# Short convolutions in token form: tap rows on VectorE and adding DMAs for the neighbour tokens

## The chip, the core and the metric

The kernel runs on one core of a Trainium2 chip. The metric is the device time of one execution in microseconds. Engines are named as the profile names them: PE (TensorE) multiplies matrices, DVE (VectorE) and ACT (ScalarE) work elementwise, POOL (GpSimd) and SP (SyncE) issue DMAs here. Each engine works through its own instructions in order.

## The reference

One encoder block over 256 tokens with 2048 channels. Two branches, gated linear attention (GLA) and a second-order Hyena operator, are gated and summed, projected, normalised, and followed by a squared-ReLU MLP. What the change touches is the start of the Hyena branch: a convolution over three neighbouring tokens for each of 6144 channels, split into v, x1 and x2.

```python
proj = h @ w_in[l]
q, k, v, r, af, ab, hy_u, gate_logits = jnp.split(proj, split_idx, axis=-1)

def _short_conv(u, w, b):          # w: (3, 6144): previous, own, next token
    y = lax.conv_general_dilated(u, w[:, None, :], (1,), [(1, 1)], ...)
    return y + b

uc = _short_conv(hy_u, conv_w, conv_b)
v, x1, x2 = jnp.split(uc, 3, axis=-1)
z = v
for o, gate in enumerate((x1, x2)):
    zc = long_convolution(z, filt[:, o])      # by FFT over 2 * 256 points
    z = gate * (zc + skip[o] * z)

merged = g0 * (y_gla @ w_gla_o) + g1 * (z @ w_hy_o)
```

## The kernel before

Activations and weights are split into a high and a low part (fp32r), and each product is the sum of three: high by high, high by low, low by high. Weights come as 305 blocks of 1 MB; `fetch` loads a block on SP's queue and splits it in two halves, high on ACT (line 84), low on DVE (line 85). Three raw blocks and three halves of each part (`whi`, `wlo`) are kept.

There are two forms of a product of 256 tokens with a block of weights. In channel form (`channel_pair`, lines 145 and 149) the weights are stationary and the result has channels on the partitions: a block gives 128 channels with 16 products 512 wide (high and low part of the activations side by side) and 16 products 256 wide. `channel_sum` (lines 157, 158) then adds the two parts: ACT takes one out of PSUM, DVE adds the other. In token form (`token_group`, lines 204 to 206) the activations are stationary and the result has tokens on the partitions: four blocks give 512 channels, with 24 products 512 wide each, straight into two PSUM tiles, one for each half of the tokens. PSUM has four such tiles in turn, so the two of one group are written again two groups later.

`pump` counts the blocks, and `later(d, f)` puts a step of the Hyena branch into the program d counts on. A scheduler then orders each engine's instructions.

The convolution stage goes over eight chunks of 256 channels. For each it makes uv, ux and uz as channel pairs of xT (tags v, x1, x2), and `short_conv` (lines 704 to 706) convolves along the free dimension, where the neighbour token is one column away: ACT scales the own token and adds the bias, DVE adds the two neighbours. v and x1 are then turned into token form by four PE transpositions each (`to_tokens`, line 713); v is split in high and low, x1 is copied out of PSUM. `hy_fwd` transforms (Zp) and loads the filter (Tl, on POOL's queue), `hy_mul` multiplies by it on DVE (Z, pa, pb, lines 754 to 760), `hy_inv` transforms back (yp), and gates with x1 in token form (line 776). After the second order the result is copied out, transposed back to channels (yT, line 786), gated with x2 in channel form (line 788), and stored to DRAM (yd, on POOL's queue), from where `reload` fetches it later. After every second chunk there is one token group of the GLA output projection (`go`). Then come the second gate (g2) and the Hyena output projection (ho).

Of the kernel before, what the change touches and what calls it, by code (L numbers as in the profile page):

```python
# [42 lines left out]
def block_kernel(  # L43
# [5 lines left out]
    wa2: bass.AP,  # L49
    ba: bass.AP,  # L50
    norm_g: bass.AP,
    convp: bass.AP,
    mlp_w: bass.AP,
    mlp_c: bass.AP,
    emb: bass.AP,
# [24 lines left out]
    def psum_side(name):  # L80
        return sdp.tile([P, 512], F32, tag="sd", name=name)

    def split_hi_lo(hi, lo, src):
        return (nc.scalar.copy(hi, src),  # L84
                nc.vector.tensor_tensor(lo, src, hi.bitcast(F32), op=ALU.subtract))  # L85
# [151 lines left out]
    conv_sb = base.tile([P, 48, 4], F32, tag="convp", name="conv_sb")  # L237
# [97 lines left out]
    def mm3(ps, lh, ll, rh, rl, start, stop):  # L335
        MM(ps, lh, rl, start=start, stop=False)
        MM(ps, lh, rh, start=False, stop=False)
        MM(ps, ll, rh, start=False, stop=stop)
# [8 lines left out]
    def filt_consts():  # L347
        raw = fp.tile([P, 4, P], F32, tag="w4", name="dftraw")
        nc.gpsimd.dma_start(raw, dft_in)
        split_hi_lo(dfth, dftl, raw)  # L350
        mw = fp.tile([P, 3, P], F32, tag="mlpw", name="mlpw")
        nc.gpsimd.dma_start(mw, mlp_w)
        mc = fp.tile([P, 4], F32, tag="mlpc", name="mlpc")
        nc.gpsimd.dma_start(mc, mlp_c)
        et = fp.tile([P, L], F32, tag="emb", name="emb_sb")
        nc.gpsimd.dma_start(et, emb)
        nc.gpsimd.dma_start(ba_sb, ba)
        nc.gpsimd.dma_start(conv_sb, convp)
# [337 lines left out]
    cst = {}  # L696
    yh_dram = {}

    def short_conv(ps, base_ct, name, tag, bufs):
        y = hp.tile([P, 2, L], F32, tag=tag, bufs=bufs, name=name)  # L700
        for c in range(2):
            cp = conv_sb[:, base_ct + c, :]
            u = ps[:, c]
            nc.scalar.activation(y[:, c, :], u, AF.Identity, scale=cp[:, 1:2], bias=cp[:, 3:4])
            nc.vector.scalar_tensor_tensor(y[:, c, 1:L], u[:, 0:L - 1], cp[:, 0:1], y[:, c, 1:L], op0=ALU.mult, op1=ALU.add)
            nc.vector.scalar_tensor_tensor(y[:, c, 0:L - 1], u[:, 1:L], cp[:, 2:3], y[:, c, 0:L - 1], op0=ALU.mult, op1=ALU.add)
        return y

    def to_tokens(src, name):
        pt = psum_side(name)  # L710
        for c in range(2):
            for tb in range(NT):
                nc.tensor.transpose(pt[:, tb * CW + c * P:tb * CW + (c + 1) * P], src[:, c, tb * P:(tb + 1) * P], ident)
        return pt.rearrange("p (a b) -> p a b", a=2)

    def z_tiles(name):
        return (hp.tile([P, NT, CW], F32R, tag="zh", bufs=2, name=f"zh{name}"),
                hp.tile([P, NT, CW], F32R, tag="zl", bufs=2, name=f"zl{name}"))
# [8 lines left out]
    def hy_x1(c):  # L727
        def run():
            x1 = hp.tile([P, NT, CW], F32, tag="x1", name=f"x1_{c}")
            nc.scalar.copy(x1, to_tokens(cst.pop(("x1c", c)), f"x1t{c}"))  # L730
            cst[("x1", c)] = x1
        return run

    def hy_fwd(c, o):
        def run():
            t = hp.tile([P, 2, 3, CW], F32, tag="Tl", name=f"Tl{c}{o}")
            nc.gpsimd.dma_start(t, T_dram[(c, o)])
            zh, zl = cst.pop(("z", c, o))
            z = hp.tile([P, 3, 2, CW], F32, tag="Z", name=f"Z{c}{o}")
            for ri in range(2):  # L740
                pz = psum_side(f"Zp{c}{o}{ri}")
                mm3(pz, dfth[:, ri], dftl[:, ri], zh, zl, True, True)
                nc.scalar.copy(z[:, 2:0:-1, ri, :], pz.rearrange("p (a b) -> p a b", a=2))
            cst[("Z", c, o)] = (t, z)
        return run
# [21 lines left out]
    def hy_inv(c, o):  # L767
        def run():
            yh, yl = cst.pop(("Y", c, o))
            py = psum_side(f"yp{c}{o}")  # L770
            py3 = py.rearrange("p (a b) -> p a b", a=2)
            mm3(py3, dfth[:, 2], dftl[:, 2], yh[:, :, 0], yl[:, :, 0], True, False)
            mm3(py3, dfth[:, 3], dftl[:, 3], yh[:, :, 1], yl[:, :, 1], False, True)
            if o == 0:
                zf = hp.tile([P, NT, CW], F32, tag="zf", name=f"zf{c}")
                nc.vector.tensor_tensor(zf, py3, cst.pop(("x1", c)), op=ALU.mult)
                z = z_tiles(f"{c}1")
                split_hi_lo(z[0], z[1], zf)
                cst[("z", c, 1)] = z
            else:  # L780
                zf = hp.tile([P, NT, CW], F32, tag="zf", name=f"zg{c}")
                nc.scalar.copy(zf, py3)
                pt = psum_side(f"yT{c}")
                for cc in range(2):
                    for tb in range(NT):
                        nc.tensor.transpose(pt[:, cc * L + tb * P:cc * L + (tb + 1) * P], zf[:, tb, cc * P:(cc + 1) * P], ident)
                yo = hp.tile([P, 2, L], F32, tag="zf", name=f"yo{c}")
                nc.vector.tensor_tensor(yo, pt.rearrange("p (a b) -> p a b", a=2), cst.pop(("x2", c)), op=ALU.mult)
                if c == NCH - 1:
                    split_hi_lo(yhT[:, 2 * c:, 0], yhT[:, 2 * c:, 1], yo)  # L790
                    return
# [12 lines left out]
        for tb in range(NT):  # L804
            nc.vector.tensor_tensor(mg[:, tb], mg[:, tb], pss[tb], op=ALU.mult)

    go_after = [0, 1, 0, 1, 0, 1, 0, 1]
    for c in range(NCH):
        ps = channel_pair(xT, f"uv{c}")
        cst[("v", c)] = short_conv(ps, 2 * c, f"cv{c}", "cv", 2)  # L810
        later(2, hy_v(c))
        later(4, hy_fwd(c, 0))
        later(4, hy_mul(c, 0))
        ps = channel_pair(xT, f"ux{c}")
        cst[("x1c", c)] = short_conv(ps, 16 + 2 * c, f"cx{c}", "cx", 1)
        later(2, hy_x1(c))
        later(6, hy_inv(c, 0))
        later(7, hy_fwd(c, 1))
        later(7, hy_mul(c, 1))
        ps = channel_pair(xT, f"uz{c}")  # L820
        cst[("x2", c)] = short_conv(ps, 32 + 2 * c, f"cz{c}", "cz", 2)
        later(9, hy_inv(c, 1))
        for _ in range(go_after[c]):
            gla_o_group()


    yhT = act_tile(base, "yT", "yh")

    def reload(c):
        def run():  # L830
            yr = hp.tile([P, 2, L], F32, tag="cv", bufs=2, name=f"yr{c}")
# [4 lines left out]
    for c in range(NCH - 1):  # L836
        later(c, reload(c))
# [289 lines left out]
def _layout(a):  # L1127
# [18 lines left out]
        seg[n] = w_in[:, s:s + z]  # L1146
        s += z
    ga = np.concatenate([seg["af"], seg["ab"]] * 4, axis=1)
    u = chan(seg["u"]).reshape(3, NCH, 2, P, D)
    go = tok(a["w_gla_o"][0])  # L1150
    ubl, gi = [], 0
    for c, n in enumerate([0, 1, 0, 1, 0, 1, 0, 1]):
        for t in range(3):
            ubl.append(u[t, c])
        ubl.append(go[gi:gi + 4 * n])
        gi += 4 * n
    f1 = chan(a["w_ff1"][0])
    w2 = a["w_ff2"][0]
    f1q = [f1[16 * i:16 * (i + 1)] for i in range(QT)]
# [18 lines left out]
    cw = a["hy_conv_w"][0].reshape(3, 48, P).transpose(2, 1, 0)  # L1178
    convp = np.concatenate([cw, a["hy_conv_b"][0].reshape(48, P).T[:, :, None]], axis=2)
# [22 lines left out]
    for r0 in (0, 32):  # L1202
# [32 lines left out]
    sc[:, 0::64] = 0.0  # L1235
    return {
        "x": a["x"][0], "first": first, "wblk": wblk, "wa2": wa2, "ba": ba, "norm_g": a["gla_norm_g"],
        "convp": convp, "mlp_w": mlp_w, "mlp_c": mlp_c, "emb": emb, "w4s": w4s,
        "ln_rows": ln_rows, "ln_turn": ln_turn, "ident_in": np.eye(P, dtype=f), "dft_in": dft,
        "sgn_in": sgn, "l2c_in": l2c, "decay_in": decay, "mask_in": mask, "scan_in": sc,  # L1240
    }
# [17 lines left out]
```

## Time and profile before

| | |
|---|---|
| median of 3 runs | 1856.17 us (1856.01 to 1856.2) |
| the profiled execution's own time | 1856.49 us |
| its span | 1854.7 us |
| instructions | 23944 |
| start of the first uv product | 457.3 us |
| start of the first go product | 531.4 us |
| start of the last uz product | 836.5 us |
| start of the last ho product | 1043.3 us |

A row of a group gives the line, engine and operation, output and inputs by the program's names, their shapes and how often it ran; then the busy time of the group and the mean of one instruction in ns; then the engine's idle time just before them and what ended it. The mean of a product is longer than the distance to the next one, since products are pipelined; distances are read from the start times of the timeline. A row of time windows gives, for each engine, busy time and instructions, then the granted clock of PE, the busy share of the DMA engines and GB/s. A row of waits gives who waited for whom, the total, how often and the longest. A row of DMA issues gives the size of one and the median time from issue to landing; a row of queues gives packets, MB and the time of its packets as a share of 16 engines' span.

### The profile page before, as it was taken

To read this page: it belongs to the slowest core of one execution; us is meant where nothing else is said; L and a number is where in the kernel's file an instruction comes from. 1 tells how busy PE (TensorE), PEld (TensorE's weight loads), DVE (VectorE), ACT (ScalarE), POOL (GpSimd) and SP (SyncE) were. 2 spreads that over 40 slices of the span, in tenths; PEclk is the share of its full clock that TensorE was granted. 3 is DMA by queue.
4 is the path that set the end of the run, shared out by engine and by line. 5 is a ranking of instruction groups with operands and counts; after the bars stand their busy time and mean duration, and the time that the engine had idled before them with its cause. 6 is when DMAs were issued, how large, how long until landed. Compare 5 with 4: busy or idle time off the path is not lost.

```text
span 1854.7 us, 23944 instructions
## 1 busy us (share of the span) xinstructions
PE 1846.9 (100%) x9447; PEld 1570.9 (85%) x9447; DVE 1286.3 (69%) x1642; ACT 935.9 (50%) x1270; POOL 29.7 (2%) x59
## 2 busy tenths in 40 slices
PE   9999999999999999999999999999999999999999
PEld 7888888888888888888888889888888888888887
DVE  6888878765788988888645567666555655665567
ACT  6656558665555555555444445444434443444332
POOL 1000000000000000000000000000000000000000
PEclk9999999999999999999999999999999999999999
DMA  8577664435555555556555764455554555555553
GB/s 317 215 250 272 239 243 169 162 136 201 196 199 202 194 205 193 207 207 227 181 203 183 277 225 167 182 214 194 182 199 187 194 192 185 201 183 193 191 191 127
DMA packets 59377, 374.99 MB, mean 202 GB/s; under 512 B 6689, under 2 KB 9153, under 8 KB 20097
## 3 DMA queue, kind: packets, MB, share of 16 engines
q1 hardware_dynamic: 46080, 324.03, 47.6%
q0 software_dynamic: 6128, 29.64, 4.3%
q10 hardware_dynamic: 7056, 19.80, 3.0%
q8 instruction: 74, 1.21, 0.3%
q14 instruction: 39, 0.31, 0.0%
HBM read 356.92 MB, written 16.52 MB: 201 GB/s over the span
## 4 chain that ended last, share of the span: by engine, by line
PE 97%; DVE 1%; ACT 1%; DMA 0%; issue 0%; SPq 0%; DVEq 0%
PE f L145 12%; PE f L149 6%; PE w L206 6%; PE w L205 6%; PE w L204 6%; PE uz L145 3%; PE uv L145 3%; PE ux L145 3%; PE g L205 3%; PE g L206 3%; PE g L204 3%; PE uv L149 2%; PE ux L149 2%; PE uz L149 2%; PE k L145 2%; PE r L206 2%
## 5 line engine op out<-in xcount | busy, mean ns | idle before, releaser
L85 DVE TENSOR_TENSOR wlo<-raw,whi 128x1024 fp32r<-128x1024 f32 x584 | 712.3, 1222 | 358.8 <-ACT whi L84 356.4
L84 ACT CAST whi<-raw 128x1024 fp32r<-128x1024 f32 x584 | 613.4, 1051 | 484.4 <-PE w L206 188.0
L145 PE MATMUL f<-hT,whi 128*128 128x512 f32 x984 | 235.1, 391 | 0.0
L145 PEld LDWEIGHTS f<-hT,whi 128*128 128x128 f32 x984 | 180.8, 188 | 35.0
L205 PE MATMUL w<-wlo,f 128*128 128x512 f32 x480 | 186.7, 389 | 0.0
L206 PE MATMUL w<-whi,f 128*128 128x512 f32 x480 | 186.7, 389 | 0.0
L204 PE MATMUL w<-whi,f 128*128 128x512 f32 x480 | 167.4, 389 | 0.0
L149 PEld LDWEIGHTS f<-hT,wlo 128*128 128x128 f32 x984 | 126.2, 191 | 4.8
L149 PE MATMUL f<-hT,wlo 128*128 128x256 f32 x984 | 127.7, 283 | 0.0
L157 ACT ACTIVATE f_l<-f 128x256 f32<-128x256 f32 x64 | 24.5, 384 | 162.2 <-PE f L145 159.3
L205 PEld LDWEIGHTS w<-wlo,f 128*128 128x128 f32 x480 | 90.1, 188 | 18.7
L204 PEld LDWEIGHTS w<-whi,f 128*128 128x128 f32 x480 | 90.1, 188 | 18.7
L206 PEld LDWEIGHTS w<-whi,f 128*128 128x128 f32 x480 | 90.1, 188 | 18.7
L205 PE MATMUL g<-wlo,xT 128*128 128x512 f32 x256 | 100.0, 391 | 0.6 <-DVE wlo L85 0.6
L158 DVE SCALAR_TENSOR_TENSOR f_s<-f,f_l 128x256 f32<-128x256 f32 x64 | 27.2, 425 | 105.1 <-ACT f_l L157 105.1
L206 PE MATMUL g<-whi,xT 128*128 128x512 f32 x256 | 99.7, 389 | 0.0
L204 PE MATMUL g<-whi,xT 128*128 128x512 f32 x256 | 92.4, 390 | 0.0
L145 PE MATMUL uz<-xT,whi 128*128 128x512 f32 x256 | 63.7, 393 | 0.0
L145 PE MATMUL ux<-xT,whi 128*128 128x512 f32 x256 | 63.6, 391 | 0.0
L145 PE MATMUL uv<-xT,whi 128*128 128x512 f32 x256 | 63.1, 391 | 0.0
L205 PEld LDWEIGHTS g<-wlo,xT 128*128 128x128 f32 x256 | 48.1, 188 | 10.9 <-DVE wlo L85 1.1
L204 PEld LDWEIGHTS g<-whi,xT 128*128 128x128 f32 x256 | 48.1, 188 | 9.9
(438 smaller groups left out, 3223.2 us busy)
## 6 DMA issues: line engine op xcount, KB each, us to landing
raw<-wblk SPq DMA_DIRECT2D x300, 1024.0 KB, 4.8
Td<-T POOLq DMA_DIRECT2D x16, 768.0 KB, 4.2
Tl<-Td POOLq DMA_DIRECT2D x16, 768.0 KB, 4.6
w<-w4s ACTq DMA_DIRECT2D x16, 512.0 KB, 4.7
xw<-first SPq DMA_DIRECT2D x5, 896.0 KB, 12.9
zr<-ln_rows ACTq DMA_DIRECT2D x4, 1024.0 KB, 10.8
xw<-first SPq DMA_DIRECT2D x6, 448.0 KB, 7.2
dec<-decay_in ACTq DMA_DIRECT2D x8, 256.0 KB, 3.7
```

The costliest lines, as they stand in the source:

```text
L84: return (nc.scalar.copy(hi, src), nc.vector.tensor_tensor(lo, src, hi.bitcast(F32), op=ALU.subtract))
L85: nc.vector.tensor_tensor(lo, src, hi.bitcast(F32), op=ALU.subtract))
L145: MM(ps[:, :, ts], hi[:, js], act[:, kt, :, ts], start=(kt == 0 and opens), stop=(kt == KT - 1))
L149: MM(ps[:, 0, ts], lo[:, js], act[:, kt, 0, ts], start=False, stop=False)
L157: nc.scalar.activation(low, ps[:, 1], AF.Copy, scale=scale)
L158: nc.vector.scalar_tensor_tensor(dst, ps[:, 0], scale, low, op0=ALU.mult, op1=ALU.add)
L204: MM(pss[tb], sh, wh, start=(kt == 0), stop=False)
L205: MM(pss[tb], sh, wl, start=False, stop=False)
L206: MM(pss[tb], sl, wh, start=False, stop=(kt == KT - 1))
```

## The change

The blocks of u are laid out for the token form, and the stage goes over four groups of 512 channels. For each it makes v, x1 and x2 by `token_group`, followed by one group of go. `short_conv` multiplies each PSUM tile three times by a row of taps that is broadcast over the partitions: for the previous token into `past`, for the next token into `ahead`, for the own token into the output `y`; then it adds the bias row. The neighbour token is now on the next partition: four DMAs on POOL's queue add `past` and `ahead` to `y`, shifted by a partition. Two of them have 127 partitions of 4096 bytes, two have one row of 2048 bytes, which crosses between the two halves of the tokens. Then the taps of the next convolution are loaded, 2048 values for each of 128 partitions. `past`, `ahead` and the taps lie in one buffer of tag G, one copy of each.

`to_tokens` and the eight steps that copied x1 are gone. v is split once for 512 channels. x2 is in token form too, so the gating comes before the transposition back, which is then only copied. The last two chunks, instead of the last one, are split into yhT directly, and six are reloaded, in buffers of tags v and x1.

```diff
-    def short_conv(ps, base_ct, name, tag, bufs):
-        y = hp.tile([P, 2, L], F32, tag=tag, bufs=bufs, name=name)
-        for c in range(2):
-            cp = conv_sb[:, base_ct + c, :]
-            u = ps[:, c]
-            nc.scalar.activation(y[:, c, :], u, AF.Identity, scale=cp[:, 1:2], bias=cp[:, 3:4])
-            nc.vector.scalar_tensor_tensor(y[:, c, 1:L], u[:, 0:L - 1], cp[:, 0:1], y[:, c, 1:L], op0=ALU.mult, op1=ALU.add)
-            nc.vector.scalar_tensor_tensor(y[:, c, 0:L - 1], u[:, 1:L], cp[:, 2:3], y[:, c, 0:L - 1], op0=ALU.mult, op1=ALU.add)
+    conv_sb = qp.tile([P, 4, 2 * 512], F32, tag="G", name="conv_sb")
+    taps = conv_sb[:, 0:2].rearrange("p a b -> p (a b)").rearrange("p (a b) -> p a b", a=4)
+    past, ahead = (conv_sb[:, 2 + i].rearrange("p (t d) -> p t d", t=NT) for i in range(2))
+
+    def load_taps(i):
+        nc.gpsimd.dma_start(conv_sb[:, 0:2].rearrange("p a b -> p (a b)"), conv_rows[i:i + 1, :].broadcast_to([P, 2048]))
+
+    def short_conv(pss, i, tag, name):
+        y = hp.tile([P, NT, 512], F32, tag=tag, name=name)
+        for tb in range(NT):
+            for j, dst in ((0, past), (2, ahead), (1, y)):
+                nc.vector.tensor_tensor(dst[:, tb], pss[tb], taps[:, j], op=ALU.mult)
+        nc.vector.tensor_tensor(y, y, taps[:, 3:4].broadcast_to([P, NT, 512]), op=ALU.add)
+        for dst, src in (
+            (y[1:P], past[0:P - 1]),
+            (y[0:1, 1], past[P - 1:P, 0]),
+            (y[0:P - 1], ahead[1:P]),
+            (y[P - 1:P, 0], ahead[0:1, 1]),
+        ):
+            nc.gpsimd.dma_start(dst, src, accum_op=ALU.add)
+        if i + 1 < 12:
+            load_taps(i + 1)
         return y
...
-    def hy_v(c):
+    def hy_v(s):
         def run():
-            z = z_tiles(f"{c}0")
-            split_hi_lo(z[0], z[1], to_tokens(cst.pop(("v", c)), f"vt{c}"))
-            cst[("z", c, 0)] = z
+            z = tuple(hp.tile([P, NT, 512], F32R, tag=t, name=f"{t}{s}") for t in ("vh", "vl"))
+            split_hi_lo(z[0], z[1], cst.pop(("v", s)))
+            for i in range(2):
+                cst[("z", 2 * s + i, 0)] = tuple(t[:, :, i * CW:(i + 1) * CW] for t in z)
         return run
...
+            zf = hp.tile([P, NT, CW], F32, tag="zf", name=f"zf{c}{o}")
+            nc.vector.tensor_tensor(zf, py3, gate_part(("x1", "x2")[o], c), op=ALU.mult)
...
-                nc.vector.tensor_tensor(yo, pt.rearrange("p (a b) -> p a b", a=2), cst.pop(("x2", c)), op=ALU.mult)
+                nc.scalar.copy(yo, pt)
...
+    load_taps(0)
+    for s in range(NCH // 2):
+        for k, n in enumerate(("v", "x1", "x2")):
+            pss = token_group(xT, f"u{n}{s}")
+            cst[(n, s)] = short_conv(pss, 3 * s + k, n, f"c{n}{s}")
+            if k == 0:
+                later(3, hy_v(s))
+                for i in range(2):
+                    c, d = 2 * s + i, 5 + 8 * i
+                    later(d, hy_fwd(c, 0))
+                    later(d, hy_mul(c, 0))
+                    later(d + 4, hy_inv(c, 0))
+                    later(d + 5, hy_fwd(c, 1))
+                    later(d + 5, hy_mul(c, 1))
+                    later(d + 9, hy_inv(c, 1))
+        gla_o_group()
```

More of the change, by code (lines that the diff above doesn't have):

```diff
@@ L51, in block_kernel @@
     norm_g: bass.AP,
-    convp: bass.AP,
+    conv_rows: bass.AP,
     mlp_w: bass.AP,
@@ L357, in filt_consts @@
         nc.gpsimd.dma_start(ba_sb, ba)
-        nc.gpsimd.dma_start(conv_sb, convp)
         nc.gpsimd.dma_start(mask_sb, mask_in)
@@ L709, in to_tokens @@
[L709 to L718, printed above, removed]
-    def hy_v(c):
+    conv_sb = qp.tile([P, 4, 2 * 512], F32, tag="G", name="conv_sb")
@@ L734, in hy_fwd, with gate_part @@
+    def gate_part(n, c):
+        return cst[(n, c // 2)][:, :, c % 2 * CW:(c % 2 + 1) * CW]
     def hy_fwd(c, o):
@@ L773, in run @@
             mm3(py3, dfth[:, 3], dftl[:, 3], yh[:, :, 1], yl[:, :, 1], False, True)
+            zf = hp.tile([P, NT, CW], F32, tag="zf", name=f"zf{c}{o}")
+            nc.vector.tensor_tensor(zf, py3, gate_part(("x1", "x2")[o], c), op=ALU.mult)
             if o == 0:
-                zf = hp.tile([P, NT, CW], F32, tag="zf", name=f"zf{c}")
-                nc.vector.tensor_tensor(zf, py3, cst.pop(("x1", c)), op=ALU.mult)
-                z = z_tiles(f"{c}1")
+                z = tuple(hp.tile([P, NT, CW], F32R, tag=t, name=f"{t}{c}") for t in ("zh", "zl"))
                 split_hi_lo(z[0], z[1], zf)
@@ L805, in gla_o_group @@
             nc.vector.tensor_tensor(mg[:, tb], mg[:, tb], pss[tb], op=ALU.mult)
[L807 to L824, printed above, removed]
+    load_taps(0)
[14 more added lines that the diff above has]
+        gla_o_group()
     yhT = act_tile(base, "yT", "yh")
@@ L830, in run @@
         def run():
-            yr = hp.tile([P, 2, L], F32, tag="cv", bufs=2, name=f"yr{c}")
+            yr = hp.tile([P, 2, L], F32, tag=("v", "x1")[c % 2], name=f"yr{c}")
             nc.gpsimd.dma_start(yr, yh_dram[c])
@@ L834, in reload @@
         return run
-    for c in range(NCH - 1):
-        later(c, reload(c))
+    for c in range(NCH - 2):
+        later(1 + 2 * c, reload(c))
     g2_sb = qp.tile([P, 4, NT, 512], F32, tag="G", name="g2_sb")
@@ L1148, in _layout @@
     ga = np.concatenate([seg["af"], seg["ab"]] * 4, axis=1)
-    u = chan(seg["u"]).reshape(3, NCH, 2, P, D)
+    u = tok(seg["u"]).reshape(3, NCH // 2, 4, P, D)
     go = tok(a["w_gla_o"][0])
[L1151 to L1156, printed above, removed]
+    ubl = []
+    for i in range(NCH // 2):
+        ubl += [u[0, i], u[1, i], u[2, i], go[4 * i:4 * i + 4]]
     f1 = chan(a["w_ff1"][0])
@@ L1177, in _layout @@
     ba = np.stack([a["gla_ba_f"][0].reshape(8, P).T, a["gla_ba_b"][0].reshape(8, P).T], axis=1)
-    cw = a["hy_conv_w"][0].reshape(3, 48, P).transpose(2, 1, 0)
-    convp = np.concatenate([cw, a["hy_conv_b"][0].reshape(48, P).T[:, :, None]], axis=2)
+    cw = np.concatenate([a["hy_conv_w"][0], a["hy_conv_b"]], axis=0)
+    conv_rows = cw.reshape(4, 3, NCH // 2, 512).transpose(2, 1, 0, 3).reshape(12, 2048)
     mlp_w = np.zeros((P, 3, P), f)
```

20 lines of the change are left out of this document (6 added, 14 removed).

## The prediction

> **What bounds the kernel now.** I read the totals of the page first, then the chain that ended last, then the stretch in which the convolutions run, cut out by time.
>
> ```profile
> span 1854.7 us, 23944 instructions
> PE 1846.9 (100%) x9447; PEld 1570.9 (85%) x9447; DVE 1286.3 (69%) x1642; ACT 935.9 (50%) x1270; POOL 29.7 (2%) x59
> PE 97%; DVE 1%; ACT 1%; DMA 0%; issue 0%; SPq 0%; DVEq 0%
> core 0: us, PE busy (x) PEld busy (x) DVE busy (x) ACT busy (x) POOL busy (x), PEclk, DMA share, GB/s
> 457.30:864.50 407.20, 407.20 (x2198) 351.99 (x2197) 351.00 (x416) 221.92 (x304) 12.87 (x24) 1.00 0.55 201
> 864.50:953.80 89.30, 89.30 (x398) 73.92 (x397) 53.47 (x51) 43.21 (x49) 2.69 (x5) 1.00 0.56 199
> ```
>
> TensorE is busy for all of the 407.2 us of the convolution stretch (457.3, the first uv product, to 864.5, the first g2 product), at a granted clock of 1.00. So a matmul or transposition taken out there comes off the time directly, as long as nothing new makes TensorE wait. VectorE is busy for 351 us of it (86%), ScalarE for 222, the DMA engines for 0.55. VectorE is where there is least room.
>
> **What comes off TensorE.** A block of weights in channel form is 16 wide and 16 half-wide products; in token form 24 wide ones. The stages of the MLP show each form alone:
>
> ```profile
> 1157.55 2.08 PE L149 MATMUL f<-hT,wlo 128*128 128x256 f32 x16
> 1159.46 3.82 PE L145 MATMUL f<-hT,whi 128*128 128x512 f32 x16
> 1163.12 2.08 PE L149 MATMUL f<-hT,wlo 128*128 128x256 f32 x16
> ...
> 1317.17 0.62 PE L204 MATMUL w<-whi,f 128*128 128x512 f32 x2
> ...
> 1319.89 0.62 PE L204 MATMUL w<-whi,f 128*128 128x512 f32 x2
> ...
> 700.78 0.60 PE L713 MATMUL x1t<-ident,cx 128*128 128x128 f32 x4
> 701.13 0.48 PE L149 MATMUL uv<-xT,wlo 128*128 128x256 f32 x2
> ```
>
> From start to start a channel block takes 1163.12 - 1157.55 = 5.57 us. From 1317.17 to 1319.89 lie 12 wide products, half a block, so a token block takes 2 x 2.72 = 5.44. Both stream the same columns; the half-wide products lose a little each. The 48 blocks of u change form: 48 x 0.13 = 6.2 us less. A set of four transpositions takes 701.13 - 700.78 = 0.35 us, and 16 sets (v and x1 of eight chunks) go: 5.6 us less. The transforms and the transposition of the result stay. Sum: 11.8 us.
>
> **VectorE and ScalarE.** Here are the groups of that stretch that go or stay, and the nearest rows to what comes.
>
> ```profile
> L706 DVE SCALAR_TENSOR_TENSOR cv<-uv_s,conv_sb,cv 128x255 f32<-128x255 f32 x16 | 7.7, 480 | 0.1
> L158 DVE SCALAR_TENSOR_TENSOR uv_s<-uv,uv_l 128x256 f32<-128x256 f32 x16 | 6.7, 421 | 13.0 <-ACT uv_l L157 13.0
> L85 DVE TENSOR_TENSOR zl<-vt,zh 128x512 fp32r<-128x512 f32 x8 | 5.5, 683 | 0.0
> L788 DVE TENSOR_TENSOR yo<-yT,cz 128x512 f32<-128x512 f32 x7 | 4.8, 684 | 0.0
> L776 DVE TENSOR_TENSOR zf<-yp,x 128x512 f32<-128x512 f32 x7 | 4.8, 692 | 3.0 <-PE yp L338 2.9
> L760 DVE TENSOR_TENSOR pa<-pa 128x1024 f32<-128x1024 f32 x15 | 18.3, 1217 | 0.0
> L85 DVE TENSOR_TENSOR wlo<-raw,whi 128x1024 fp32r<-128x1024 f32 x129 | 156.8, 1221 | 22.4 <-ACT whi L84 21.9
> L754 DVE TENSOR_TENSOR Z<-Z 128x512 f32<-128x512 f32 x15 | 10.3, 689 | 1.3 <-ACT Z L743 1.0
> L755 DVE TENSOR_TENSOR pa<-Z,Tl 128x1536 f32<-128x1536 f32 x15 | 26.3, 1756 | 0.3
> L757 DVE TENSOR_TENSOR pa<-pa,pb 128x768 f32<-128x768 f32 x15 | 14.3, 952 | 0.1
> L704 ACT ACTIVATE cv<-uv_s,conv_sb 128x256 f32<-128x256 f32 x16 | 9.6, 599 | 0.0
> L157 ACT ACTIVATE uv_l<-uv 128x256 f32<-128x256 f32 x16 | 6.1, 384 | 37.1 <-PE uv L145 37.1
> L730 ACT COPY x<-x1t 128x512 f32<-128x512 f32 x8 | 4.8, 594 | 1.2 <-PE x1t L713 1.2
> ```
>
> Gone from VectorE: 96 side taps like L706 at 0.48 (46.1 us; L705 has the same shape), 48 channel sums at 0.42 (20.2), 8 splits of v at 0.68 (5.5) and 8 gatings at L788 (5.5): 77.3 us. Come: 72 products of a PSUM row with a row of taps, 128x512 with one operand in PSUM as in L776, at 0.69 (49.7); 12 additions of the bias over 1024 columns at 1.22 (14.6, by L760); 4 splits of v of 1024 columns (4.9); 8 gatings with x2 at 0.69 (5.5): 74.7. VectorE stays where it is; in a stretch 12 us shorter it is some 88% busy. ScalarE loses 48 x 0.60 and 48 x 0.38 and the 8 copies of x1, about 52 us. The waits of uv_s for uv_l (13.0 us in its row) go too. None of this is on TensorE's path on average.
>
> In bursts it may be. A convolution is one block of 6 x 0.69 + 1.22 = 5.4 us. In the changed kernel's order VectorE has, behind a weight half in the third and fourth group of columns, the v split (1.22), Z (0.69), pa and pb (1.76 each), a weight half (1.22), six tap products of x1 (6 x 0.69) and the next half (1.22): 12.0 us from the end of one half to the end of the second after it. With three buffers for the halves, TensorE can be kept three halves of 2.72 us ahead, 8.2 us; it needs that second half after 3 + 1 halves, at 10.9 us, or 12.3 when the six products of a transform (6 x 0.23) fall between. So such a place costs 0 to 1.1 us; after it pa twice (0.95 each) and a half arrive every 3.1 us against 2.7, some 0.5 more. Of such places there are at most twelve, one per convolution: 0 to about 20 us. I take 2 us, since TensorE never waited behind the same chain of Z, pa and pb before, with VectorE as busy.
>
> **The DMAs that add.** Each convolution puts five transfers on POOL's queue: two adds of 127 partitions x 4096 B (0.52 MB), two adds of one row, and the next taps (1 MB). No add, and no transfer of 127 partitions, stands in the trace. The nearest rows:
>
> ```profile
> q0 software_dynamic: 6128, 29.64, 4.3%
> Td<-T POOLq DMA_DIRECT2D x16, 768.0 KB, 4.2
> yd<-yo POOLq DMA_DIRECT2D x7, 256.0 KB, 2.4
> raw<-wblk SPq DMA_DIRECT2D x300, 1024.0 KB, 4.8
> L462 POOL DMA_DIRECT2D Td<-T x16 | 8.5, 533 | 220.8 <-DVE T L460 220.8
> POOL Tl L737 <- DVE pb L756: 319.0, 15, 71.1
> ```
>
> Lower end: between yd and Td, 512 KB more take 1.8 us, so 508 KB land in 2.4 + 0.9 = 3.3 us. If the add has to bring its target too, the moving part doubles: 1.5 fixed + 2 x 1.8 = 5.1. Upper end: all of it through one of the 16 engines. The queue took 4.3% of 16 x 1854.7 us, 1276 engine-us, for 29.64 MB, 43 us per MB; 0.52 MB are 22.4 us, or 44.8 with the target read as well.
>
> The queue's waits hold up all behind them: Tl waited 319 us there for buffers, in order. In the new order the second row add and the second large add wait for the first large one, since they touch the same bytes of y; the Tl loads, yd stores and yr reloads stand behind. So a convolution's chain is 0.5 issue + add + 0.5 + add: 7.6 to 11.2 us at the low prices. The first to need it is vl on VectorE (vh on ScalarE), with the weight halves queued behind both, and then TensorE. Between the bias addition and vl stand five to seven halves, at least 5 x 2.72 = 13.6 us. The products into ahead, which wait for the adds of the convolution before, have five halves or more as well; x1 has eight or more, x2 more still. Taps arrive with the adds, 4.8 us by the raw row. So at the low prices all of it is hidden, and I cost it at nothing; the cover is used up at an add of about 6.3 us. I take the low end, because every POOL transfer of the trace moves at the speed of many engines: Td's 768 KB would need 34 us on one, and landed in 4.2. The bytes added (at most 38 MB to the 82 MB of the stretch) bring the DMA share from 0.55 to about 0.8, still under a block's time for a weight block.
>
> The Trainium skill speaks against that. Its page "DMA: Bandwidth & Descriptors", section "Why a DMA increments its semaphore by 16 and not by 1", states that a DMA uses the largest number of engines up to 16 that divides the slowest dimension of both sides, so that 127 partitions go to one engine; it also reports an exception, some direct copies issued from GpSimd with 127 partitions on all 16. Whether an adding DMA has that exception it does not say, and no run here shows it: by the rule the sum would be that of the second rival, by the exception that of the forecast.
>
> **Sum.** Against the execution's own 1856.5 us (the span 1854.7 and 1.8 around it): 1856.5 - 11.8 + 2 = 1846.7; the median of the runs is 0.3 below that execution, so 1846.4.
>
> **Rivals.**
> - VectorE's bursts decide. At 1.6 us for each of twelve convolutions TensorE loses 19 us: 1864. For it: VectorE at 88%. Against it: no wait of TensorE behind equal bursts before. It decides from 1 us per convolution, where the gain is gone.
> - One engine carries each large add (slower, the other side). At 22.4 + 1.5 + 0.5 = 24.4 us an add, a convolution can't follow the last before 5.4 + 2 x 24.4 = 54.2 us. Twelve of these from 479 (457.3 and one group of 21.8) end at 1129; the reader of the last x2, the gating of chunk 6, would stand at about 875 in the forecast (g2 begins at 864.5 - 11.8 = 853, its go group 21.8 earlier at 831, the last tap products end near 837, then come 14 halves). So 254 late, less 8 of halves in hand: about 2093. With the target read through the same engine, 46.8 an add and 99 a convolution: end at 1667, about 2630. It decides from 6.3 us an add. For it: the shape is new to this queue, and no row tells how it is shared out; against it: every POOL row so far.
> - The add spreads but costs more than its bytes, say 10 us: a chain of 21 us against 13.6 leaves 7.4 per convolution, or 2 to 7 after the halves in hand; 12 of them give 1870 to 1930.
>
> **How the numbers follow.** Forecast 0.40, its own range 1842 (no burst at all, and a block 0.05 us faster still than the two paces tell, 48 times) to 1852. VectorE's bursts 0.14, up to 1869. The costly spread add 0.10. One engine 0.36, of which 0.20 at the single price and 0.16 at the double. A measurement of this kernel tells 0.2%, 3.7 us, from no change. Faster is the forecast, 0.40; the bursts split into 0.06 same and 0.08 slower; the rest is slower: 0.54 in all. The range 1842 to 2140 holds 0.84; only the double price is left out.
>
> **What would show it.** Right: the convolution stretch near 397 us with TensorE busy throughout, token blocks of u at 5.44, adds landing in 3 to 6 us, vl waiting for no DMA. Wrong at the adds: large adds landing in 20 us or more, VectorE idle at vl or ahead released by a DMA, TensorE idle behind weight halves, POOL's queue full. Wrong at VectorE: TensorE idle by 1 to 2 us after tap products with no DMA named.

## The result, and the profile after

The changed kernel takes 1907.35 us (median of 4 runs, 1903.43 to 1907.68) against 1856.18 (1856.01 to 1856.48): a ratio of 1.0271, 95% interval 1.0253 to 1.0288. It is 51 us slower where 10 us faster was forecast; the time lies in the range (1842 to 2140).

Totals of the profile after, the slices of its clock, and the chain that ended last:

```profile
span 1905.3 us, 22925 instructions
PE 1853.6 (97%) x8999; PEld 1553.2 (82%) x8999; DVE 1284.3 (67%) x1578; ACT 893.8 (47%) x1160; POOL 76.2 (4%) x116
PEclk9999999999999999988999999999999999999999
PE 76%; DMA 8%; DVE 7%; issue 6%; ACT 1%; POOL 1%; SPq 0%; DVEq 0%; POOLq 0%; ACTq 0%
```

Before, the chain was 97% PE. Now DMAs, VectorE and issues have 21% of it, and the granted clock dips in two slices in the middle. The windows of the convolution stretch (cut at 905, just ahead of the first g2 product at 909.5) and of what follows:

```profile
457.50:905.00 447.50, 403.22 (x1704) 325.71 (x1703) 331.40 (x333) 171.76 (x185) 58.24 (x79) 0.95 0.75 229
905.00:995.00 90.00, 90.00 (x402) 74.46 (x401) 67.41 (x66) 46.15 (x54) 3.84 (x7) 1.00 0.58 210
```

Before, TensorE was busy for all of the stretch; now it stands still for 447.5 - 403.2 = 44.3 us of it, and the clock is 0.95. Behind it TensorE is busy throughout again. VectorE is not the bound: 331 of 447.5 us. From the first uv to the first ho product it is 546.8 us where it was 496.5, so all but 0.3 of the 50.6 us by which the span grew lie there. The DMA issues show what is new:

```profile
cx<-conv_sb POOLq DMA_DIRECT2D x16, 508.0 KB, 8.2
cv<-conv_sb POOLq DMA_DIRECT2D x8, 508.0 KB, 9.9
cx<-conv_sb POOLq DMA_DIRECT2D x16, 2.0 KB, 7.0
conv_sb<-conv_rows POOLq DMA_DIRECT2D x12, 1024.0 KB, 13.0
```

By these medians a large add lands in 8.2 to 9.9 us (forecast 3.3 to 5.1), a row add in 7.0, the taps in 13.0 (forecast 4.8). But each median of the large adds mixes two kinds. Taken issue by issue, the first large add of a convolution lands in 6.9 to 9.2 us (median 7.5), the second in 8.6 to 13.5 (median 11.2). The same row cut out for the first convolution, its first add and then its second:

```profile
cv<-conv_sb POOLq DMA_DIRECT2D x1, 508.0 KB, 9.2
cv<-conv_sb POOLq DMA_DIRECT2D x1, 508.0 KB, 10.7
```

The weight loads slow down too. Their row from 457 to 905, with 4.8 us in the same stretch before the change:

```profile
raw<-wblk SPq DMA_DIRECT2D x64, 1024.0 KB, 7.4
```

Waits of the same execution: who waited for whom, total, times, longest.

```profile
ACT vh L84 <- DMA cv<-conv_sb: 34.3, 4, 9.9
DVE vl L85 <- ACT vh L84: 24.1, 3, 9.7
DVE conv_sb L708 <- DMA cx<-conv_sb: 18.5, 4, 5.6
ACT whi L84 <- DMA raw<-wblk: 31.4, 11, 6.0
PE go L205 <- DVE wlo L85: 24.6, 4, 7.6
PE Zp L335 <- DVE vl L85: 7.8, 2, 3.9
```

These are the readers that the prediction named: the v split waits for the adds of v (all four times), and the products into `ahead` for those of the convolution before. VectorE and ScalarE then stand at that instruction with weight halves queued behind, and TensorE waits for `wlo`.

The first convolution shows the chain. POOL's timeline (start, duration, instruction, in brackets the idle time before it), then VectorE's:

```profile
485.22 1.73 POOL L716 DMA_DIRECT2D cv<-conv_sb  x2 [57.11 <-DVE cv L709]
486.31 1.22 POOL L702 DMA_DIRECT2D conv_sb<-conv_rows  x1
494.68 1.65 POOL L716 DMA_DIRECT2D cv<-conv_sb  x2 [7.15 <-DMA cv<-conv_sb]
```

```profile
483.69 1.22 DVE L709 TENSOR_TENSOR cv<-cv,conv_sb 128x1024 f32<-128x1024 f32 x1
...
506.21 0.69 DVE L708 TENSOR_TENSOR conv_sb<-ux,conv_sb 128x512 f32<-128x512 f32 x1 [4.79 <-DMA cv<-conv_sb]
...
507.41 1.22 DVE L85 TENSOR_TENSOR vl<-cv,vh 128x1024 fp32r<-128x1024 f32 x1
```

The first add is issued at 485.22, right after the bias. The second pair has to wait for its landing and starts at 494.68, with the row add, and the large add follows at 495.45. The 1 MB of taps is issued between them, on the same queue: in the packet records of the trace the packets of the taps run from 493.07 to 499.32, and the first packet of the second large add starts at 499.63. At 506.21, 21.0 us after the first issue, VectorE may go on. The cover was worked out as 13.6 us.

At x2 the same happens with the adds of x1, and there VectorE has nothing else to do. VectorE, then TensorE, in the second group:

```profile
639.38 0.69 DVE L708 TENSOR_TENSOR conv_sb<-ux,conv_sb 128x512 f32<-128x512 f32 x1 [2.16 <-DMA conv_sb<-conv_rows]
645.65 0.69 DVE L708 TENSOR_TENSOR conv_sb<-ux,conv_sb 128x512 f32<-128x512 f32 x1 [5.58 <-DMA cx<-conv_sb]
...
649.78 2.35 DVE L85 TENSOR_TENSOR wlo<-raw,whi 128x1024 fp32r<-128x1024 f32 x2
```

```profile
651.05 0.80 PE L205 MATMUL go<-wlo,yg 128*128 128x512 f32 x1 [7.46 <-DVE wlo L85]
...
652.50 0.63 PE L206 MATMUL go<-whi,yg 128*128 128x512 f32 x1
652.92 0.63 PE L204 MATMUL go<-whi,yg 128*128 128x512 f32 x1
...
655.60 0.39 PE L206 MATMUL go<-whi,yg 128*128 128x512 f32 x1
655.82 0.39 PE L205 MATMUL go<-wlo,yg 128*128 128x512 f32 x1
```

VectorE waits 2.16 us for the late taps and 5.58 for the adds, and the next half is ready 7.46 us after TensorE wanted it. And behind this wait the products come 0.43 us apart, at a granted clock of 0.5, and only from 654.2 on 0.23. There are seven such phases. Windows of TensorE alone, over its work inside a phase (length, busy time with products, clock, DMA share, GB/s), of the first, the third and the last:

```profile
538.24:541.65 3.41, 3.41 (x10) 0.51 0.58 161
...
651.05:654.29 3.24, 3.24 (x8) 0.51 0.25 63
...
888.61:893.20 4.59, 4.59 (x11) 0.50 0.51 175
```

The seven hold some 77 products, 8 to 17 each, in 30.7 us of TensorE's busy time. At full clock they would take about half: some 15 us are lost. So the 51 us are made up of 44.3 us of standing still and some 15 at half clock, less the 11.8 that were gained, which makes some 48. The remaining 3 us were not traced to a cause.

### The profile page after: what moved, and what is told of

Its sections match the earlier page's. It is cut to its first block, busy times and chain, and to the rows that moved or that the text cites. A ratio compares the mean times of both kernels' runs of the same rounds, so it can differ in the third digit from the quotient of the medians.

```text
span 1905.3 us, 22925 instructions
## 1 busy us (share of the span) xinstructions
PE 1853.6 (97%) x8999; PEld 1553.2 (82%) x8999; DVE 1284.3 (67%) x1578; ACT 893.8 (47%) x1160; POOL 76.2 (4%) x116
## 4 chain that ended last, share of the span: by engine, by line
PE 76%; DMA 8%; DVE 7%; issue 6%; ACT 1%; POOL 1%; SPq 0%; DVEq 0%; POOLq 0%; ACTq 0%
PE f L145 12%; PE f L149 6%; PE w L205 6%; PE w L206 6%; PE w L204 6%; DMA cx<-conv_sb 4%; DMA cv<-conv_sb 4%; PE g L205 3%; PE g L206 3%; PE g L204 3%; DVE wlo L85 2%; PE ho L205 2%; PE ho L204 2%; PE ho L206 2%; PE go L205 1%
## 5 line engine op out<-in xcount | busy, mean ns | idle before, releaser
L205 PE MATMUL ux<-wlo,xT 128*128 128x512 f32 x256 | 103.5, 404 | 7.3 <-DVE wlo L85 7.1
L206 PE MATMUL ux<-whi,xT 128*128 128x512 f32 x256 | 101.9, 398 | 0.0
L204 PE MATMUL ux<-whi,xT 128*128 128x512 f32 x256 | 92.6, 396 | 4.6 <-ACT whi L84 2.9
L205 PE MATMUL go<-wlo,yg 128*128 128x512 f32 x128 | 53.8, 421 | 24.6 <-DVE wlo L85 24.6
L205 PEld LDWEIGHTS ux<-wlo,xT 128*128 128x128 f32 x256 | 49.4, 193 | 22.9 <-DVE wlo L85 12.8
```

The costliest lines, as they stand in the source:

```text
L204: MM(pss[tb], sh, wh, start=(kt == 0), stop=False)
L205: MM(pss[tb], sh, wl, start=False, stop=False)
L206: MM(pss[tb], sl, wh, start=False, stop=(kt == KT - 1))
```

## The experiments

The first four kernels each take one thing out of the changed kernel, so each leaves part of the computation out. The kernel before took 1858.17 us beside them (one run; the other runs of it have medians of 1856.2 to 1857.0).

**No adds at all.** All four adds of a convolution are gone, so the neighbour tokens are missing.

```diff
-            nc.gpsimd.dma_start(dst, src, accum_op=ALU.add)
```

> Leaves out the four adding DMAs of every convolution, so the neighbour tokens are missing from v, x1 and x2; the taps are still loaded and all products of VectorE are made. Theory (the chain of adds holds VectorE and ScalarE up): all of the loss goes, 1844 to 1850 us, no wait of TensorE over 1 us in the convolution stretch. Rival (VectorE's bursts): the waits before go and behind the tap products stay, 1875 us or more. Rival (traffic delays the weight loads): part of it stays with the 12 loads of taps, 1860 to 1880.

1846.19 us: 12.0 below that run of the kernel before, 10.0 below the median of 1856.18, and 61 below the changed kernel. The window of its convolution stretch:

```profile
457.30:853.00 395.70, 394.17 (x1743) 324.22 (x1743) 336.64 (x340) 177.42 (x190) 16.52 (x31) 1.00 0.63 233
```

TensorE is busy for all but 1.5 us, at full clock, with every tap product, bias and split still on VectorE. From the first uv to the first ho product its busy time is 484.7 us where it was 496.5: 11.8 less, the sum that was forecast. So the new form is worth what was forecast, VectorE's bursts cost next to nothing, and all of the loss comes with the adds.

**Only the adds of the past token.** The next token is missing.

```diff
-            (y[0:P - 1], ahead[1:P]),
-            (y[P - 1:P, 0], ahead[0:1, 1]),
```

> Leaves out the two DMAs that add the next token; the previous token is added and the taps are loaded. Half of the adds' bytes, and no second add to wait for the first. Theory (the serial chain): a chain of 8 to 10 us fits into the 13.6 us of cover, 1844 to 1855 us. Rival (traffic): half of the loss stays, 1870 to 1880. Rival (bursts): 1890 or more.

1850.13 us. One large add (7.5 to 8.0 us to landing) costs 4 us in all; the second, which has to wait for it, costs the other 57. So one add all but fits under the cover (the v split still waits 14.0 us for it, but little of that reaches TensorE), and two in a chain do not.

**The taps loaded once.** Convolutions 2 to 12 use the taps of the first.

```diff
-        if i + 1 < 12:
-            load_taps(i + 1)
```

> All twelve convolutions use the taps of the first one, which are loaded once; the adds stay. In the changed kernel the second large add lands some 20 us after the bias addition, and 5 us of that are the 1 MB of taps between the two on POOL's queue. Theory: chains of 14 to 16 us, TensorE's waits fall from 49 us to 10 to 25, time 1860 to 1880. Rival (the adds' own length alone): above 1890. Rival (bursts): unchanged, 1900 or more.

1892.89 us. The taps between the two adds cost 14 us; the larger part stays, as the rival said. DMA issues and waits:

```profile
cx<-conv_sb POOLq DMA_DIRECT2D x16, 508.0 KB, 7.3
ACT vh L84 <- DMA cv<-conv_sb: 30.8, 4, 11.8
```

Without the 1 MB between them the first add lands in 7.1 us in the median (7.5 in the changed kernel) and the second in 9.2 (11.2), and the v split still waits for them.

**Overwriting instead of adding.** The same four transfers without the addition, so the shifted values take the place of the sum.

```diff
-            nc.gpsimd.dma_start(dst, src, accum_op=ALU.add)
+            nc.gpsimd.dma_start(dst, src)
```

> The same four DMAs overwrite y instead of adding to it, so the sum of the three tokens is not formed. Tells the price of adding from that of moving. Theory: a packet of 4096 B falls from 327 ns to some 160, a large transfer lands in about 5 us instead of 8.2, the chain is some 14 us (taps still between), time 1855 to 1880. If the fixed part of the GpSimd queue rules instead, landing stays above 7 us and the time above 1890.

1884.78 us, a little over what was expected. DMA issues:

```profile
cx<-conv_sb POOLq DMA_DIRECT2D x16, 508.0 KB, 7.0
cv<-conv_sb POOLq DMA_DIRECT2D x8, 508.0 KB, 7.6
```

These medians mix the two kinds too. In the first convolution the second pair can be issued 5.6 us after the first, where it took 9.5 with adding:

```profile
485.33 1.04 POOL L716 DMA_DIRECT2D cv<-conv_sb  x2 [57.10 <-DVE cv L709]
...
490.90 0.49 POOL L716 DMA_DIRECT2D cv<-conv_sb  x1 [3.98 <-DMA cv<-conv_sb]
```

Over all twelve, the first plain transfer lands in 5.3 us in the median, where the first add took 7.5; the second, behind the taps, lands in 10.7, where the add took 11.2. So the addition makes a transfer that has no taps ahead of it 2.2 us longer, and the kernel without it is 22.6 us faster. A plain first transfer stays under the 6.3 at which the cover is used up, the first add doesn't. The pair doesn't fit in either form: from the first issue to the last landing it takes 17.4 us in the median, 19.8 with adding, against a cover of 13.6.

The next kernels compute all of it. They move things, to bring the chain back under its cover. The kernel before took 1856.53 us (median of 7 runs) beside the first four.

**Taps on SP's queue.**

```diff
-        nc.gpsimd.dma_start(conv_sb[:, 0:2].rearrange("p a b -> p (a b)"), ...)
+        nc.sync.dma_start(conv_sb[:, 0:2].rearrange("p a b -> p (a b)"), ...)
```

> Computes all; only the loads of taps go from POOL's queue to SP's. Theory (two adds in series, some 8 us each): the taps no longer lie between them, but one run without their loads was still at 1893, so 1880 to 1900 us, and waits for adds at vh and at the products into ahead stay. Rival (taps are the trouble): 1860 or less.

1875.09 us, 32 less than the change and better than expected: more than leaving the taps out had saved. The second add now lands in 7.0 us in the median, and the first, which has the taps beside it on the other queue, in 10.9, so the chain of the two is hardly shorter (18.9 us from 19.8). What is shorter are two waits of ScalarE: the one for weights falls from 31.4 to 9.6 us, and that of the v split from 34.3 to this:

```profile
ACT vh L84 <- DMA cv<-conv_sb: 19.6, 4, 6.4
```

Why they fall so far is not settled; it is a single run, as is the one with the taps left out.

**The v split and all that follows two blocks later.**

```diff
-                later(3, hy_v(s))
+                later(5, hy_v(s))
-                    c, d = 2 * s + i, 5 + 8 * i
+                    c, d = 2 * s + i, 7 + 8 * i
```

> Computes all; the split of v and all transforms behind it come two blocks (11 us) later, nothing else changes. Theory: vh and vl wait for no add any more, but the products of x2 into ahead still wait for the adds of x1, which is the larger part of TensorE's waits (25 of 49 us): 1870 to 1890 us. Rival (v alone is the trouble): below 1860.

1898.75 us, a miss. The scheduler hardly moved the split: ScalarE still waited 28.2 us for the adds of v.

**The own token and the bias first, then past with its adds, then ahead.**

```diff
+        for tb in range(NT):
+            nc.vector.tensor_tensor(y[:, tb], pss[tb], taps[:, 1], op=ALU.mult)
+        nc.vector.tensor_tensor(y, y, taps[:, 3:4].broadcast_to([P, NT, 512]), op=ALU.add)
+        for j, dst, pairs in ((0, past, ...), (2, ahead, ...)):
+            for tb in range(NT):
+                nc.vector.tensor_tensor(dst[:, tb], pss[tb], taps[:, j], op=ALU.mult)
+            for to, src in pairs:
+                nc.gpsimd.dma_start(to, src, accum_op=ALU.add)
```

> Computes all; the own token and the bias come first on VectorE, then the products into past with their two adds, then those into ahead with theirs; taps stay on POOL's queue. The first large add can start before the products into ahead and doesn't wait for a late bias addition. Theory: the chain ends 3 to 6 us earlier, 1870 to 1890 us. Rival (no earlier end, since the adds are in series behind the taps): 1900 or more.

1891.37 us, just over the range and 16 us less than the change. The reason given beforehand isn't what happened: in the trace the bias addition still comes after the products into past and ahead, and the first add is issued 0.3 us after the bias, as in the changed kernel (3.7 us behind the last product in the median, where it was 4.8). Where the 16 us come from is not shown.

**These three together.**

> Computes all; taps on SP's queue, own token and bias first, v split and transforms two blocks later. Theory: the two adds end some 18 us after the products into past, within the 22 us of a group, and TensorE's waits go: 1844 to 1852 us, below the kernel before. Rival (traffic on the DMA engines, or bursts on VectorE): above 1858.

1880.43 us (median of 4, 1878.52 to 1886.46), ratio 1.0118 (1.01 to 1.0136): far over the 1844 to 1852 expected, and no better than the taps on SP's queue alone. New waits have come:

```profile
ACT whi L84 <- DMA raw<-wblk: 42.6, 13, 6.4
DVE pa L753 <- DMA Tl<-Td: 12.9, 2, 6.8
```

The weights come late (31.4 us of such waits in the changed kernel), and the filter loads Tl stand on POOL's queue behind an add that waits.

**The v split forced back.** Since the scheduler had not moved it, it is now tied behind the newest weight half, beside the two blocks of the run above. In the program it stands 11 halves behind the bias instead of 5.

```diff
+            with tc.issue_after(newest[0].ins), tc.issue_after(newest[1].ins):
                 split_hi_lo(z[0], z[1], cst.pop(("v", s)))
```

> Computes all; the changed kernel with the split of v queued behind the weight halves five blocks later, eleven halves after the bias addition where five stood, and the transforms two blocks later. Theory: no wait of vh or vl for adds (34 us of ScalarE's and 24 of VectorE's idle time before), the waits of the products into ahead stay, and late weight loads too: 1875 to 1895 us. Rival (the wait of v is the whole trouble): below 1860. Rival (the waits only move to ahead): 1900 or more.

1886.41 us (before: 1856.35), as expected: 21 us saved. The wait of the v split for the adds is gone from the list, and the next reader has taken its place:

```profile
DVE conv_sb L709 <- DMA cv<-conv_sb: 19.9, 4, 6.4
PE go L206 <- DVE wlo L85: 13.6, 3, 5.0
```

**All of these together**, and then **with Tl on ScalarE's queue as well**:

> Computes all; own token and bias first, taps on SP's queue, and the split of v held eleven halves behind. Left are the Tl loads on POOL's queue, which stand behind the adds (two waits of 6.8 us for Tl in the run with all three edits). Theory: 1855 to 1875 us. Rival (traffic on the DMA engines): above 1878, with ScalarE waiting 40 us for weight loads.

> Computes all; as the run before it, and the Tl loads are issued by ScalarE, so that nothing but adds, stores and reloads stands on POOL's queue. Theory: no wait behind an add is left on VectorE or ScalarE, 1846 to 1854 us, below the kernel before. Rival (traffic delays the weight loads): above 1858, with waits for weight loads over 20 us.

```diff
-            nc.gpsimd.dma_start(t, T_dram[(c, o)])
+            nc.scalar.dma_start(t, T_dram[(c, o)])
```

1874.03 us, at the upper end of the range, and 1865.99 us (median of 4, 1863.22 to 1868.72), ratio 1.0053 (1.0036 to 1.0069). The second missed its 1846 to 1854: it is the best complete form that was tried, 41 us under the changed kernel and still 9.6 over the one before. Its waits and issues:

```profile
SPq L703 <- DVE cx L709: 42.3, 7, 9.7
SPq L703 <- DVE cv L709: 30.5, 4, 9.5
ACT whi L84 <- DMA raw<-wblk: 37.2, 11, 5.2
conv_sb<-conv_rows SPq DMA_DIRECT2D x12, 1024.0 KB, 6.3
cx<-conv_sb POOLq DMA_DIRECT2D x16, 508.0 KB, 10.0
```

SP waits 72.8 us for the convolutions to be done with the old taps (L703), with weight loads queued behind. That looked like what was left.

**The next taps behind one or two more weight loads.** Only their place among SP's loads differs from the last kernel.

```diff
+    def next_taps(i):
+        with tc.issue_after(newest[2].ins):
+            load_taps(i)
...
         if i + 1 < 12:
-            load_taps(i + 1)
+            later(3, lambda: next_taps(i + 1))
```

(4 in place of 3 in the second.)

> As e9_tl_act, with the load of the next taps put behind one more weight load on SP's queue at nine of its eleven places. Theory: what e9 still loses comes from SP waiting 72.8 us for the convolutions to finish with the old taps before it may load the new ones, which holds up the weight loads behind (ScalarE waits 33.7 us for raw there). One load later takes part of that away: 1855 to 1863 us, SP's waits for the taps 30 to 60 us. Rival, the length of the adds and their traffic remain: 1863 to 1870, as e9.

> As e9_tl_act, with the load of the next taps put behind two more weight loads on SP's queue at ten of its eleven places. Theory as for e13_taps_next1: SP hardly waits for the taps (under 25 us), ScalarE's wait for late weights under 15 us, 1847 to 1858 us. Rival, the length of the adds and their traffic remain: 1863 to 1870. A second rival: the taps now come too late for the next convolution, VectorE waits for conv_rows, and the time is over 1865.

1873.12 us (1870.07 to 1874.3; ratio 1.0081, 1.0064 to 1.0097) and 1867.81 us (1866.99 to 1869.28; 1.0053, 1.0036 to 1.007): both over what was expected, the first also over its rival's 1870. Waits and issues of the second:

```profile
SPq L703 <- DVE cx L713: 1.4, 2, 0.7
conv_sb<-conv_rows SPq DMA_DIRECT2D x12, 1024.0 KB, 12.1
ACT whi L84 <- DMA raw<-wblk: 30.5, 11, 4.8
```

The theory fell: SP's waits are gone, the weights come nearly as late as they did (30.5 us for 37.2; 56.8 in the first of the two), and no time is won. The taps' load now stands right behind a weight load and lands in 12.1 us instead of 6.3, and VectorE waits 4.3 us for it, so part of the second rival came true. The waits of SP were not the main thing that held up the weights. Without adds the same wait of ScalarE for weights is 4.6 us, before the change 4.8. With all four adds it lies anywhere from 9.0 us (taps loaded once) to 56.8, so the adds alone don't set it either; what else does is open.

**What the price of an add hangs on.** Two kernels that leave out or misplace neighbours: in the first, one add of all 128 partitions without a shift, then one of the next token for the first 128 tokens alone; in the second, the row adds alone. The kernel before took 1857.0 us beside them.

```diff
+        nc.gpsimd.dma_start(y, past, accum_op=ALU.add)
+        nc.gpsimd.dma_start(y[0:P - 1, 0], ahead[1:P, 0], accum_op=ALU.add)
```

> As after, but of the four adds of a convolution two are left, and both add the wrong tokens: the first adds all 128 partitions without a shift (512 KB), the second the next token of the first half of the tokens alone (127 partitions, 254 KB). It measures what the price of an add hangs on. If it is the shape of 127 partitions, the first lands in 3.3 to 5.1 us, as the prediction worked out from yd and Td. If it is the bytes, the first lands in about 8 and the second in 4 to 5. If most of it doesn't depend on the bytes, the second lands in 6.5 us or more. The time is between that of the run with one add and that of after: 1850 to 1900 us.

```diff
+        nc.gpsimd.dma_start(y[0:1, 1], past[P - 1:P, 0], accum_op=ALU.add)
+        nc.gpsimd.dma_start(y[P - 1:P, 0], ahead[0:1, 1], accum_op=ALU.add)
```

> As after, with the two row adds of 2 KB alone; the two large adds are left out, so only the tokens at the seam of the two halves have their neighbours. It measures an add that has hardly any bytes and stands behind no large one. If the 7 us of a row add in after are its own, it lands in 6 to 7 us here too, and the time is some us over the run without adds (1848 to 1855). If it only lands behind the large one on its queue, it lands in 2 to 3 us, and the time is that of the run without adds, 1845 to 1848 us.

1861.42 us and 1845.43 us. DMA issues of the first kernel (its add without a shift, then the shifted half), then of the second:

```profile
cx<-conv_sb POOLq DMA_DIRECT2D x8, 512.0 KB, 6.1
cx<-conv_sb POOLq DMA_DIRECT2D x8, 254.0 KB, 7.9
```

```profile
cx<-conv_sb POOLq DMA_DIRECT2D x16, 2.0 KB, 3.4
```

A 2 KB add without a large one ahead lands in 3.4 us, not 7: in the changed kernel it lands with the large add or the taps ahead of it. The two large adds of the first kernel can't be set against each other, since the second has the taps ahead of it on the queue. Each can be set against the add in the same place of the changed kernel. The first: 512 KB over 128 partitions without a shift land in 6.4 us in the median (all twelve), 508 KB over 127 with a shift in 7.5. So the shape of 127 shifted partitions accounts for some 1.1 us (the row add beside it is gone too), and the rest of the distance to the 3.3 to 5.1 that were forecast is not the shape. The second: 254 KB land in 7.9, 508 KB in 11.2, so behind the taps the bytes do count. None of the three outcomes named beforehand came out cleanly.

The first kernel also shows a chain that costs time while the weights come in time. Its two adds take 14.8 us from the first issue to the last landing, just over the cover of 13.6, and ScalarE waits only 4.7 us for weights. It is 15 us over the run without adds, and the v split waits 17.6 us for its adds.

## Why the prediction was wrong

- **What bounds the kernel.** Right. Without adds the time falls with TensorE's work, by 10 to 12 us. (The first g2 product stands at 862.2 in the trace before, not at 864.5; no term hangs on it.)
- **What comes off TensorE.** Right: 11.8 us forecast, and without adds TensorE's busy time falls by 11.8, from 496.5 to 484.7.
- **VectorE and ScalarE.** Right in the sum: 1284.3 us busy on VectorE against 1286.3 before (2.6 less were forecast). The bursts were priced at 2 us; without adds TensorE stands 1.5 us in the whole stretch. The rival in which they decide falls. ScalarE's busy total fell by 42 us where some 52 were given, without effect on the time.
- **The DMAs that add.** This is the step that failed: "I take the low end", 3.3 to 5.1 us an add, and so "I cost it at nothing". In the median the first add of a convolution measured 7.5 and the second 11.2, both over the 6.3 that the prediction itself gave as the limit of the cover. The price had been scaled from yd and Td, which share neither the route nor the addition: a plain transfer of this form lands in 5.3 where 3.3 were scaled, the addition makes it 7.5, and the taps ahead of the second add bring that to 11.2. The row it was scaled from doesn't hold still either: yd lands in 5.6 us here and in 5.1 without adds, where it was 2.4. The chain was given as 7.6 to 11.2 us and is 19.8 in the median, 21.0 at the first convolution: 9.5 to the second issue, the rest to its landing.
- **The taps.** "Taps arrive with the adds, 4.8 us": they land in 13.0, they stand between the two adds, and taking them out is worth 14 us. The sum of the chain left them out.
- **The readers.** Right: v's split and the products into ahead, with the halves behind them, and then TensorE. Where the first reader was put off, the next one waited.
- **Weights.** "Still under a block's time for a weight block": wrong in the stretch. The DMA share is 0.75 where 0.8 was forecast, but a weight block lands in 7.4 us in the median, over the block's 5.44, and weights come late (31.4 us of ScalarE's waits against 4.8). Without adds it lands in 4.9 at the same GB/s (230), so it is the adds that slow the weight loads, not the bytes moved as a whole.
- **One engine.** Wrong: at 508 KB in 7.5 us against the 22.4 of one engine the adds are spread. The packet records show it directly: the first add of all has 127 packets of 4096 bytes with 79 us of packet time inside 7.0 us, so eleven at once on average. The Trainium skill's rule for 127 partitions ("DMA: Bandwidth & Descriptors", section "Why a DMA increments its semaphore by 16 and not by 1") doesn't hold for these adds; they behave as the exception that it reports for some direct copies from GpSimd.
- **The costly spread add.** This rival is closest to what happened: its chain of 21 us is the one measured, and its 1870 to 1930 us hold the time. It was given 0.10. But its two equal adds of 10 us are really 7.5 and 11.2, the second with the taps ahead of it, and it has no term for the half clock, some 15 of the 51 us: that its range holds the time is in part luck. The unknown price was bounded by 3.3 and 44.8 us, with the limit of the cover at 6.3, close to the low end: the fault was to take that end on the strength of rows that share neither the route nor the addition.

What remains open: why the best complete form is still 9.6 us over the kernel before, some 20 over the run without adds. In its profiled execution 3.0 us of this lie ahead of the convolutions (the first uv product starts at 460.3, after a wait of TensorE and a half-clock phase near 138 us). The rest isn't SP's wait for the taps. Late weights are likely part of it: in the stretch a block lands in 7.5 us (no adds: 4.9), at a DMA share of 0.80 (no adds: 0.63). But a run with the same traffic and no chain wasn't made.

## What to carry to other kernels

Where the price of a new operation is unknown and the limit of its cover lies inside the bounds, ask first on which side of that limit it falls, and don't take an end of the bounds because other transfers on the same queue sit there. Transfers that touch the same bytes form a chain: count each landing, each issue, and what the scheduler may put on the queue between them (here 21 us, where one transfer alone cost 4 us of time). Before a median of landings is compared, ask whether its transfers stand in the same place on their queue. And put off one reader of such a chain only if the next reader can wait as well.

## What was not expected of the hardware

A wait of TensorE can cost more than its length. After waits of 2.1 to 7.6 us the granted clock was 0.5 for 3.4, 6.8 or 10.2 us, some 15 us in seven such phases. The Trainium skill ("TensorE: Matmul & The Clock Gate", section "What's actually happening") gives a window of 3.413 us that runs freely, and the phases here are one, two and three of these. The same page of the Trainium skill ("TensorE: Matmul & The Clock Gate", section "HAM oscillation — how this bites in real kernels") warns of gaps over about 3.4 us; here one of 2.10 us was enough, before the phase that the first of the windows above shows. Nor does the length of a wait decide alone: with overwriting in place of adding a wait of 3.07 us had no such phase behind it. The product that ended the wait of 2.10 us:

```profile
537.56 0.50 PE L205 MATMUL go<-wlo,yg 128*128 128x512 f32 x1 [2.10 <-DVE wlo L85]
```
